# Low limbs of gathered tokens: one one-hot matrix and a copy by ScalarE, in place of a second one-hot matrix and a third product

## The chip, the cores and the metric

The kernel runs on one core of a Trainium2 chip. A core has TensorE (PE: matrix products into PSUM), VectorE (DVE), ScalarE (ACT), GpSimd (POOL) and SyncE (SP), whose queue here issues the transfers (DMA) from main memory. Each engine works through its own list of instructions in order and waits on semaphores for the others. The metric is the time of one execution on the device in microseconds (us); lower is better. Before the change it is 1878.24 us, the median of 3 runs (1877.51 to 1880.09).

## The reference, cut to what matters

A two-layer network on 256 latent tokens of width 1024, with 256 context tokens. The second layer ends in a mixture of eight experts, and the change lies there:

```
logits = (t @ w_router).astype(float32)          # t: 256 tokens x 1024
topv, topi = lax.top_k(logits, 2)
wts = softmax(topv, axis=-1)
combine = sum(wts[..., None] * one_hot(topi, 8), axis=1)
y = zeros_like(t)
for e in range(8):
    y = y + combine[:, e:e + 1] * ((silu(t @ w_g[e]) * (t @ w_u[e])) @ w_d[e])
```

w_g and w_u are 1024 x 3584 for each expert, w_d is 3584 x 1024, all in float32. After it come a gated residual and a final RMSNorm.

## The kernel before, in words

**Limbs.** Products of float32 values are made from two rounded parts: a value is its high limb (what is left of it in the fast product format) plus its low limb (the rest). A product of two tensors is then three products: high with high, low with high, high with low. For weights a load brings 1 MB, a unit, into a buffer `raw`; ScalarE writes the high limbs `eh` (line 1362, `Flow.high`) and VectorE the low limbs `el` = raw - eh (line 1386, `Flow.low`). When a unit's low limbs are made, its buffer is given back (`Flow.release`) and SyncE's queue may issue the next load. `Flow.take(look)` is called by each unit's products: it makes sure of that unit's limbs, and has `look` units more split in advance.

**Tokens of an expert.** The kernel gathers the tokens that go to an expert as the columns of a tile `xh` (with low limbs in `xlo`; for some experts both are halves of one tile `x`), 128 columns wide, with a product by a one-hot matrix `d` (`gather`, line 1443): th (high limbs of all tokens) times `d`, and tl (low limbs) times `d`. When an expert has at most 64 tokens (`FEW`), columns 64 to 127 of `xh` hold the low limbs of the same tokens, so one product with `xh` does the work of two; the two halves of the result are added later (`fold`, and line 1997 for the activations). With more than 64 tokens there is a separate product with `xlo`. For the low limbs in those columns the kernel builds a second one-hot matrix `dl`, with the positions moved by 64 and only for experts with few tokens, and adds the product tl times `dl` to the same result. The later transposed matrix `dT`, with which an expert's output is scattered back to the tokens, is made from `dl` + `d` (line 1479), so that it has the one of each token twice.

The choice between few and many is made while the kernel runs: the counts are loaded into registers of PE, DVE and ACT (`load_count`), and `tc.If(tokens[e] > FEW)` makes a branch on these engines, also on one that has nothing to do inside. In the profile, experts 3, 5 and 6 run the separate product with `xlo`, and the other five don't.

**Order.** Experts run in turn; each has four blocks of its hidden width (1024, 1024, 1024, 512), and a block takes gate units, up units, and the down units of the block before it. Gathers are generators that are advanced a step at a time between units (`bgq["attn"]`, `tick`): expert 1's during expert 0, those of 2 and 3 together during expert 1, of 4 and 5 during expert 3, of 6 and 7 during expert 5. A step makes one chunk's product: four of the eight rows of 128 features for one expert, two for a pair. The first gather is the exception: its steps stand by hand, some ahead of the first unit, some inside it (`mid`, between a unit's high and low products) and behind it.

Of the kernel before, what the change touches and what calls it, by code (L numbers as in the profile page):

```python
# [11 lines left out]
F32 = mybir.dt.float32  # L12
# [3 lines left out]
OP = mybir.AluOpType  # L16
# [59 lines left out]
def hybrid_kernel(ctx, tc, x, c, ctx_in, c_ctx, w_mod, b_mod, norm1_g, norm2_g, w_in, sink, w_fourier,  # L76
# [1347 lines left out]
    w_shift = cmp[:, 0]  # L1424
    d0, dl0 = (rawx.tile([128, 2, 128], F32R, name=nm, bufs=1) for nm in ("d0", "dl0"))
    xl = xT[:, :, 256:512].rearrange("p c (t i) -> p c t i", t=2)
# [7 lines left out]

    def one_hot(d, e, low=False):
        at, on = (posl, sel_few) if low else (pos, sel)
        for t in range(2):
            V.tensor_scalar(d[:, t, :], slot, at[:, t, e:e + 1], on[:, t, e:e + 1],
                            op0=OP.is_equal, op1=OP.mult)
# [3 lines left out]
    def gather(es, base, info):  # L1443


        d, dl, w = d0, dl0, 128 * len(es)
        if es[0] > 1 or base:
            d, dl = (ex.tile([128, 2, 256], F32R, name=nm, tag=tag, bufs=1) for nm, tag in
                     (("d", "ych"), ("dl", "ycl")))
        if es[0] or base:  # L1450
            for i, e in enumerate(es):
                one_hot(d[:, :, i * 128:i * 128 + 128], e)
                if not base:
                    one_hot(dl[:, :, i * 128:i * 128 + 128], e, True)
        yield
# [6 lines left out]
        nk = 512 // w  # L1462
        of = ([(th, d)] + ([] if base else [(tl, dl)]), [(tl, d)])
        for ch in range(0, KC, nk):
            for l in range(2):
                p = psB.tile([128, nk, w], F32, name="pg", tag="t", bufs=2)
                for src, dd in of[l]:
                    for k in range(nk):
                        for t in range(2):
                            P_.matmul(p[:, k, :], src[:, t, (ch + k) * 128:(ch + k + 1) * 128], dd[:, t, :w],  # L1470
                                      start=(src is of[l][0][0] and k + t == 0),
                                      stop=(src is of[l][-1][0] and k + t == nk))
                for i, e in enumerate(es):
                    A.activation(info[e]["x"][l][:, ch:ch + nk, :], p[:, :, i * 128:i * 128 + 128], AF.Copy)  # L1474
                yield
        if base:
            dl = d
        else:
            V.tensor_tensor(dl[:, :, :w], dl[:, :, :w].bitcast(F32), d[:, :, :w].bitcast(F32), op=OP.add)
        if late_weights:  # L1480
# [5 lines left out]
        for i, e in enumerate(es):  # L1486
            di = dl[:, :, i * 128:i * 128 + 128].bitcast(F32)
            p = psB.tile([128, 512], F32, name="pd", tag="t", bufs=2)
            for t in range(2):
                P_.transpose(p[:, t * 128:(t + 1) * 128], di[:, t, :], ident)  # L1490
            for t in range(2):
                P_.matmul(p[:, 256:257], di[:, t, :], comb[:, t, e:e + 1], start=(t == 0), stop=(t == 1))
            dT = ex.tile([128, 256], F32R, name="dT", tag="dT", bufs=3)
            cs = mp.tile([128, 1], F32, name="cs", tag="cs", bufs=3)
            A.activation(dT, p[:, 0:256], AF.Copy)
            A.activation(cs, p[:, 256:257], AF.Copy)
            info[e].update(dT=dT, cs=cs)
            yield

    with ExitStack() as st:  # L1500
# [33 lines left out]
        def row(dst, dg):  # L1534
# [16 lines left out]
        tl = mp.tile([128, 2, D], F32R, name="tl")  # L1551
        sel, comb, rank, sel_few = (mp.tile([128, 2, NE], F32, name=nm) for nm in
                                    ("sel", "comb", "rank", "sel_few"))
        posl = rank
        most = mp.tile([128, 1], I32, name="most")
# [3 lines left out]
        pos = at_of[:, 0:2, :]  # L1559
        few = mp.tile([128, NE], F32, name="few")  # L1560
        gate_cols(1, 2, 0.5, 1)
# [100 lines left out]
        normed(0)  # L1662
        V.tensor_scalar(few, at_of[:, 2, :], FEW + 0.5, None, op0=OP.is_lt)
        V.tensor_scalar(posl, pos, 64.0, None, op0=OP.add)
        V.tensor_tensor(sel_few, sel, few[:, None, :].to_broadcast([128, 2, NE]), op=OP.mult)
        one_hot(dl0, 0, True)
        low_limbs(0)
# [4 lines left out]
        next(g0)  # L1672
        load_count(0)
        next(g0)
        flow.high()
# [11 lines left out]
    with ExitStack() as st:  # L1687
# [121 lines left out]
        def experts(base, flow):  # L1809
# [88 lines left out]
            for j in range(end + 1):  # L1898
                if j < end:
# [3 lines left out]
                    if j == NB and base == 0:  # L1903
                        bgq["attn"].append(rows_of_gates())
                    if b == 1 and e + 1 < NE and base == 0:
                        load_count(e + 1)
                    if j == 2:
# [9 lines left out]
                    for br, ps in enumerate((pg, pu)):  # L1917
                        nu = KC // nk
                        for q in range(nu):
                            unit(e, [(ps[:, h:h + 512], q * nk + k, k * wd + h)  # L1920
                                     for k in range(nk) for h in range(0, wd, 512)],
                                 xh, xlo, q == 0, q == nu - 1, 0 if j == 0 and br == 0 and q == 0 else 2,
                                 br or j == 0 or q < nu - 1,
                                 (lambda: next(g)) if j == 0 and br == 0 and q < 2 and not base else None)
                            if j == 0 and br == 0:
                                if q == 0 or base and q == 1:
                                    next(g)
# [102 lines left out]
```

## Time and profile before

| | |
|---|---|
| median of 3 runs | 1878.24 us |
| profiled execution, its time | 1877.18 us |
| its span (first to last instruction) | 1875.5 us |
| busy: PE, DVE, ACT | 1790.7, 1517.4, 1143.0 us |
| products `dl` with tl | 80 |

The span is 1.7 us shorter than the execution's time. In a timeline row the columns are: start, length, engine, line, operation, out<-in, shapes, count, and in brackets how long the engine was idle before it and what ended that. Rows of one operation that follow each other are merged, and products are pipelined, so their lengths overlap; the distance between two starts is what a group took. PEclk in a row of stretches is the granted TensorE clock: 1.00 is 2.4 GHz and 0.50 is 1.2 GHz. A row of waits gives who waited for whom, the total in us, how often, and the longest.

### The profile page before, as it was taken

To read this page: it belongs to the slowest core of one execution; us is meant where nothing else is said; L and a number is where in the kernel's file an instruction comes from. 1 tells how busy PE (TensorE), PEld (TensorE's weight loads), DVE (VectorE), ACT (ScalarE), POOL (GpSimd) and SP (SyncE) were. 2 spreads that over 40 slices of the span, in tenths; PEclk is the share of its full clock that TensorE was granted. 3 is DMA by queue.
4 is the path that set the end of the run, shared out by engine and by line. 5 is a ranking of instruction groups with operands and counts; after the bars stand their busy time and mean duration, and the time that the engine had idled before them with its cause. 6 is when DMAs were issued, how large, how long until landed. Compare 5 with 4: busy or idle time off the path is not lost. (4 is left out here: it accounts for less than half of the span.)

```text
span 1875.5 us, 27319 instructions
## 1 busy us (share of the span) xinstructions
PE 1790.7 (95%) x9701; PEld 1497.7 (80%) x9701; DVE 1517.4 (81%) x1793; ACT 1143.0 (61%) x1300; POOL 64.3 (3%) x95
## 2 busy tenths in 40 slices
PE   7999999999999999999989999999999999999996
PEld 4788877878888888999878777778887788888874
DVE  6787896577778636787698988999889998888897
ACT  5664623433232224665497877888777887777785
POOL 3200000200000002000000000000000000000000
PEclk9999999999999999999899999999999999999999
DMA  9313462266467422535799999999999999999993
GB/s 295 108 57 102 130 202 95 80 210 199 158 224 249 158 94 85 158 95 209 276 361 339 394 367 361 408 403 408 344 352 405 399 400 327 346 353 375 370 401 123
DMA packets 223312, 488.57 MB, mean 261 GB/s; under 512 B 11426, under 2 KB 107938, under 8 KB 223140
## 3 DMA queue, kind: packets, MB, share of 16 engines
q1 hardware_dynamic: 221860, 482.11, 71.2%
q0 software_dynamic: 1280, 4.20, 0.8%
q8 instruction: 105, 1.72, 0.4%
q14 instruction: 67, 0.55, 0.1%
HBM read 485.22 MB, written 1.05 MB: 259 GB/s over the span
## 5 line engine op out<-in xcount | busy, mean ns | idle before, releaser
L1386 DVE TENSOR_TENSOR el<-raw,eh 128x2048 fp32r<-128x2048 f32 (+2 forms) x332 | 724.0, 2210 | 86.0 <-ACT eh L1362 77.5
L1362 ACT ACTIVATE eh<-raw 128x2048 fp32r<-128x2048 f32 (+2 forms) x332 | 607.8, 1859 | 95.3 <-PE pgt L1843 63.5
L212 PE MATMUL psp<-hh,wh 128*128 128x512 f32 (+1 forms) x704 | 258.9, 368 | 2.6 <-ACT U L965 1.8
L214 PE MATMUL psp<-hh,wl 128*128 128x512 f32 (+1 forms) x704 | 255.1, 362 | 5.4 <-DVE wl L181 5.4
L213 PE MATMUL psp<-hl,wh 128*128 128x512 f32 (+1 forms) x704 | 254.4, 361 | 0.0
L181 DVE TENSOR_TENSOR wl<-raw,wh 128x1024 fp32r<-128x1024 f32 (+1 forms) x152 | 182.4, 1206 | 32.8 <-issue 13.1
L169 ACT ACTIVATE wh<-raw 128x1024 fp32r<-128x1024 f32 (+1 forms) x152 | 156.8, 1039 | 48.8 <-DMA raw<-in_w_down_d 20.4
L214 PEld LDWEIGHTS psp<-hh,wl 128*128 128x128 f32 x704 | 132.9, 189 | 28.3 <-DVE wl L181 8.0
L212 PEld LDWEIGHTS psp<-hh,wh 128*128 128x128 f32 x704 | 133.2, 189 | 25.0 <-issue 2.2
L213 PEld LDWEIGHTS psp<-hl,wh 128*128 128x128 f32 x704 | 133.2, 189 | 19.6 <-issue 0.5
L1843 PE MATMUL py<-el,eah 128*128 128x256 f32 (+1 forms) x712 | 125.9, 315 | 8.6 <-DVE el L1386 7.3
L1843 PEld LDWEIGHTS py<-el,eah 128*128 128x128 f32 x712 | 102.0, 189 | 36.6 <-DVE el L1386 28.3
L1843 PE MATMUL py<-eh,eah 128*128 128x512 f32 x440 | 120.8, 396 | 0.0
L331 DVE SCALAR_TENSOR_TENSOR acc<-rawm,cvec,acc 128x512 f32<-128x512 f32 x140 | 99.8, 746 | 1.3
L1843 PE MATMUL pup<-el,xh 128*128 128x256 f32 (+1 forms) x560 | 93.6, 305 | 4.7 <-DVE el L1386 4.6
L1843 PEld LDWEIGHTS pup<-el,xh 128*128 128x128 f32 x560 | 80.0, 188 | 20.2 <-DVE el L1386 11.5
L1843 PE MATMUL pgt<-el,xh 128*128 128x256 f32 (+1 forms) x480 | 84.5, 314 | 11.2 <-DVE el L1386 10.7
L1843 PE MATMUL pup<-eh,xh 128*128 128x512 f32 x336 | 94.4, 402 | 0.0
L1843 PEld LDWEIGHTS pgt<-el,xh 128*128 128x128 f32 x480 | 69.7, 191 | 27.7 <-DVE el L1386 19.6
L1843 PEld LDWEIGHTS py<-eh,eah 128*128 128x128 f32 x440 | 78.6, 188 | 14.6 <-ACT eh L1362 0.8
L1843 PE MATMUL pgt<-eh,xh 128*128 128x512 f32 x296 | 84.1, 406 | 0.7 <-ACT xh L1474 0.7
L1207 ACT ACTIVATE ah<-af 128x512 fp32r<-128x512 f32 x22 | 13.9, 632 | 95.1 <-DVE af L1206 95.1
(382 smaller groups left out, 3242.6 us busy)
## 6 DMA issues: line engine op xcount, KB each, us to landing
raw<-in_w_gate_e SPq DMA_DIRECT2D x111, 1024.0 KB, 8.1
raw<-in_w_down_e SPq DMA_DIRECT2D x110, 1024.0 KB, 8.3
raw<-in_w_up_e SPq DMA_DIRECT2D x109, 1024.0 KB, 8.8
rawm<-in_w_mod SPq DMA_DIRECT2D x112, 256.0 KB, 4.9
raw<-in_w_in SPq DMA_DIRECT2D x26, 1024.0 KB, 5.5
raw<-in_w_gate_d SPq DMA_DIRECT2D x11, 1024.0 KB, 5.4
raw<-in_w_up_d SPq DMA_DIRECT2D x11, 1024.0 KB, 5.4
mraw<-in_w_mod SPq DMA_DIRECT2D x16, 512.0 KB, 8.5
```

Source lines behind the costliest of these rows:

```text
L169: A.activation(h[:, :n, :], src, AF.Copy)
L181: self.eng.tensor_tensor(lo[:, :n, :], src, h[:, :n, :].bitcast(F32), op=OP.subtract)
L212: P_.matmul(ps, wh[:, k, :], ah, start=(start and i == 0), stop=False)
L213: P_.matmul(ps, wh[:, k, :], al, start=False, stop=False)
L214: P_.matmul(ps, wl[:, k, :], ah, start=False, stop=(stop and i == n - 1))
L331: V.scalar_tensor_tensor(acc[v], r, s, acc[v], op0=OP.mult, op1=OP.add)
L1207: A.activation(ah[:, i, :], t, AF.Copy)
L1362: A.activation(self.like(self.hi[i][:, sl], x), x, AF.Copy)
L1386: V.tensor_tensor(self.like(self.lo[i][:, sl], x), x, self.like(self.hi[i][:, sl], x).bitcast(F32), op=OP.subtract)
L1843: P_.matmul(ps[:, a:b], x[:, k, :], w[:, c + a:c + b], start=(start and ps_id[i] not in seen), stop=(stop and ps_id[i] not in ps_id[i + 1: ...
```

## The change

`dl`, `few`, `sel_few` and the moved positions are gone, with their one-hot steps and the sum of `dl` and `d`. A gather's chunk is now two products, th with `d` and tl with `d`. For the second, ScalarE branches: with many tokens it copies to `xlo` as before; with few it copies the first 64 columns into columns 64 to 127 of `xh`. `dT` and `cs` are written in two halves of 64 rows; with few tokens the second half is a second copy of the first. The counts of experts e+1 and e+2 are now read together in every odd expert, since a pair's gather asks for both. In the first gather, both products of chunk 0 stand ahead of the first unit and those of chunk 1 inside units 0 and 1; the first unit now looks two units ahead, as all others do.

```
-    d0, dl0 = (rawx.tile([128, 2, 128], F32R, name=nm, bufs=1) for nm in ("d0", "dl0"))
+    d0 = rawx.tile([128, 2, 128], F32R, name="d0", bufs=1)
...
                 one_hot(d[:, :, i * 128:i * 128 + 128], e)
-                if not base:
-                    one_hot(dl[:, :, i * 128:i * 128 + 128], e, True)
...
-        of = ([(th, d)] + ([] if base else [(tl, dl)]), [(tl, d)])
...
+            for l, src in enumerate((th, tl)):
...
+                for k in range(nk):
+                    for t in range(2):
+                        P_.matmul(p[:, k, :], src[:, t, (ch + k) * 128:(ch + k + 1) * 128], d[:, t, :w],
+                                  start=(k + t == 0), stop=(k + t == nk))
                 for i, e in enumerate(es):
-                    A.activation(info[e]["x"][l][:, ch:ch + nk, :], p[:, :, i * 128:i * 128 + 128], AF.Copy)
+                    pe, (hi, lo) = p[:, :, i * 128:i * 128 + 128], info[e]["x"]
+                    if l == 0 or base:
+                        A.activation((hi, lo)[l][:, cs_, :], pe, AF.Copy)
+                        continue
+                    with tc.If(tokens[e] > FEW) as many:
+                        A.activation(lo[:, cs_, :], pe, AF.Copy)
+                    with many.Else():
+                        A.activation(hi[:, cs_, 64:128], pe[:, :, 0:64], AF.Copy)
                 yield
-        if base:
-            dl = d
-        else:
-            V.tensor_tensor(dl[:, :, :w], dl[:, :, :w].bitcast(F32), d[:, :, :w].bitcast(F32), op=OP.add)
...
-            di = dl[:, :, i * 128:i * 128 + 128].bitcast(F32)
+            di = d[:, :, i * 128:i * 128 + 128].bitcast(F32)
...
-            A.activation(dT, p[:, 0:256], AF.Copy)
-            A.activation(cs, p[:, 256:257], AF.Copy)
+            def rows(to, src):
+                A.activation(dT[to], p[src, 0:256], AF.Copy)
+                A.activation(cs[to], p[src, 256:257], AF.Copy)
...
+                with tc.If(tokens[e] > FEW) as many:
+                    rows(first, first)
+                    rows(second, second)
+                with many.Else():
+                    rows(first, first)
+                    rows(second, first)
...
         next(g0)
         load_count(0)
+        next(g0)
         next(g0)
...
-                    if b == 1 and e + 1 < NE and base == 0:
-                        load_count(e + 1)
+                    if b == 1 and base == 0:
+                        for e1 in ((1,) if e == 0 else (e + 1, e + 2) if e % 2 and e + 2 < NE else ()):
+                            load_count(e1)
...
-                                 xh, xlo, q == 0, q == nu - 1, 0 if j == 0 and br == 0 and q == 0 else 2,
+                                 xh, xlo, q == 0, q == nu - 1, 2,
...
-                                if q == 0 or base and q == 1:
+                                if base and q < 2:
                                     next(g)
```

What ScalarE has in a row at the first gather and the first units, before (`xh` and `xlo` are copies of the gather's chunks, `th` the high limbs of the second half of the features, the first `eh` is half of unit 1, the last row units 2 and 3 and so on; the branch is a unit's):

```order
L1474 ACTIVATE xh<-pg 128x512
L1362 ACTIVATE eh<-raw 128x1024
L1651 ACTIVATE th<-xa 128x512 x2
L1474 ACTIVATE xlo<-pg 128x512
L1868 COMPARE_AND_BRANCH
L1868 UNCONDITIONAL_BRANCH x2
L1474 ACTIVATE xh<-pg 128x512
L1362 ACTIVATE eh<-raw 128x2048 x2
L1474 ACTIVATE xlo<-pg 128x512
```

The same place on ScalarE, now:

```order
L1470 ACTIVATE xh<-pg 128x512
L1472 COMPARE_AND_BRANCH
L1473 ACTIVATE xlo<-pg 128x512
L1472 UNCONDITIONAL_BRANCH
L1475 ACTIVATE xh<-pg 128x4x64
L1472 UNCONDITIONAL_BRANCH
L1362 ACTIVATE eh<-raw 128x1024
L1657 ACTIVATE th<-xa 128x512 x2
L1362 ACTIVATE eh<-raw 128x2048
L1470 ACTIVATE xh<-pg 128x512
```

The second copy of chunk 0 has come ahead of unit 1's half, and unit 2's `eh` ahead of the copy of chunk 1.

TensorE at the same place, before (`pg` is the gather's result, `pgt` the gate's):

```order
L1470 MATMUL pg<-d_6322,th 128x128 x8
L1470 MATMUL pg<-dl_6323,tl 128x128 x8
L1843 MATMUL pgt<-eh,xh 128x512 x4
L1470 MATMUL pg<-d_6322,tl 128x128 x8
L1868 COMPARE_AND_BRANCH
L1843 MATMUL pgt<-eh,xlo 128x512 x4
L1843 MATMUL pgt<-el,xh 128x512 x4
L1868 UNCONDITIONAL_BRANCH
L1843 MATMUL pgt<-el,xh 128x256 x8
L1868 UNCONDITIONAL_BRANCH
L1470 MATMUL pg<-d_6322,th 128x128 x8
L1470 MATMUL pg<-dl_6323,tl 128x128 x8
```

And now:

```order
L1465 MATMUL pg<-d_6322,th 128x128 x8
L1465 MATMUL pg<-d_6322,tl 128x128 x8
L1472 COMPARE_AND_BRANCH
L1472 UNCONDITIONAL_BRANCH x2
L1846 MATMUL pgt<-eh,xh 128x512 x4
L1465 MATMUL pg<-d_6322,th 128x128 x8
L1871 COMPARE_AND_BRANCH
L1846 MATMUL pgt<-eh,xlo 128x512 x4
L1846 MATMUL pgt<-el,xh 128x512 x4
L1871 UNCONDITIONAL_BRANCH
L1846 MATMUL pgt<-el,xh 128x256 x8
L1871 UNCONDITIONAL_BRANCH
```

Two groups of eight products stand ahead of the first unit as before, but the second is now `d,tl`; inside unit 0 the first of chunk 1 stands in the place of the last of chunk 0; and a branch with no work in it has come onto TensorE.

VectorE at the gather of experts 2 and 3, before:

```order
L1438 TENSOR_SCALAR d<-cols,at_of,sel 128x128 x2
L1438 TENSOR_SCALAR dl<-cols,rank,sel_few 128x128 x2
L1438 TENSOR_SCALAR d<-cols,at_of,sel 128x128 x2
L1438 TENSOR_SCALAR dl<-cols,rank,sel_few 128x128 x2
L1385 COMPARE_AND_BRANCH
L1386 TENSOR_TENSOR el<-raw,eh 128x2048
L1385 UNCONDITIONAL_BRANCH x2
```

And now:

```order
L1437 TENSOR_SCALAR d<-cols,at_of,sel 128x128 x4
L1385 COMPARE_AND_BRANCH
L1386 TENSOR_TENSOR el<-raw,eh 128x2048
L1385 UNCONDITIONAL_BRANCH x2
L1871 COMPARE_AND_BRANCH
```

The four steps of `dl` are gone from the front of the next `el`.

## Rows read from the trace of the kernel before

**Rows 1.** Stretches: busy us and count of PE, PEld, DVE, ACT, POOL; clock; DMA share, GB/s

```profile
944.00:990.00 46.00, 40.80 (x240) 32.58 (x239) 44.33 (x36) 43.02 (x36) 0.00 (x0) 1.00 1.00 377
1262.00:1390.00 128.00, 128.00 (x612) 105.58 (x611) 112.46 (x72) 98.39 (x83) 0.00 (x0) 1.00 0.98 367
1490.00:1750.00 260.00, 260.00 (x1209) 212.32 (x1208) 227.15 (x136) 197.62 (x151) 0.00 (x0) 1.00 0.96 361
```

**Rows 2.** Waits, 900 us and 925 us to the end: the queue's, VectorE's for weights

```profile
SPq L1236 <- DVE el L1386: 682.7, 265, 12.9
...
DVE el L1386 <- DMA raw<-in_w_gate_e: 1.8, 2, 1.4
```

**Rows 3.** Timeline of TensorE at the first gather and units 0 to 3

```profile
929.34 2.07 PE L1843 MATMUL pgt<-eh,xh 128*128 128x512 f32 x4 [0.75 <-ACT xh L1474]
931.21 1.80 PE L1470 MATMUL pg<-d,tl 128*128 128x128 f32 x8
932.81 2.00 PE L1843 MATMUL pgt<-el,xh 128*128 128x256 f32 x8
934.62 1.03 PE L1470 MATMUL pg<-d,th 128*128 128x128 f32 x8
935.49 1.06 PE L1470 MATMUL pg<-dl,tl 128*128 128x128 f32 x8
...
941.36 1.21 PE L1843 MATMUL pgt<-el,xh 128*128 128x256 f32 x8 [1.10 <-DVE el L1386]
942.40 1.10 PE L1843 MATMUL pgt<-eh,xh 128*128 128x512 f32 x4
```

**Rows 4.** Timeline of ScalarE and of VectorE at the same place

```profile
930.13 1.14 ACT L1651 ACTIVATE th<-xa 128x512 fp32r<-128x512 f32 x2
...
937.07 3.71 ACT L1362 ACTIVATE eh<-raw 128x2048 fp32r<-128x2048 f32 x2
...
939.01 6.70 DVE L1386 TENSOR_TENSOR el<-raw,eh 128x2048 fp32r<-128x2048 f32 x3 [5.99 <-ACT eh L1362]
```

**Rows 5.** Stretches at the start and after the second gather

```profile
926.00:934.00 8.00, 7.25 (x31) 6.68 (x31) 5.73 (x10) 3.18 (x5) 0.00 (x0) 0.50 0.17 38
...
940.00:944.00 4.00, 2.84 (x17) 2.06 (x16) 4.00 (x3) 4.00 (x4) 0.00 (x0) 1.00 0.62 199
1010.00:1018.00 8.00, 7.44 (x44) 6.29 (x45) 6.48 (x6) 8.00 (x8) 0.00 (x0) 1.00 0.55 186
```

**Rows 6.** Timeline of TensorE and ScalarE at the gather of expert 1

```profile
991.42 1.06 PE L1470 MATMUL pg<-dl,tl 128*128 128x128 f32 x8
992.31 3.70 PE L1843 MATMUL pgt<-raw,xh 128*128 128x172 f32 x24
...
992.51 0.60 ACT L1474 ACTIVATE xh<-pg 128x512 fp32r<-128x512 f32 x1 [2.48 <-PE pg L1470]
```

**Rows 7.** Timeline of three engines where the gather of 2 and 3 ends

```profile
1133.32 0.68 DVE L1479 TENSOR_TENSOR dl<-dl,d 128x512 fp32r<-128x512 f32 x1
...
1134.15 0.41 PE L1490 MATMUL pd<-ident,dl 128*128 128x128 f32 x2 [2.96 <-DVE dl L1479]
...
1134.94 0.39 ACT L1495 ACTIVATE dT<-pd 128x256 fp32r<-128x256 f32 x1 [2.65 <-PE pd L1492]
...
1138.55 0.38 ACT L1495 ACTIVATE dT<-pd 128x256 fp32r<-128x256 f32 x1 [1.36 <-PE pd L1492]
```

**Rows 8.** Timeline of TensorE in expert 3

```profile
1343.80 0.64 PE L1470 MATMUL pg<-dl,tl 128*128 128x256 f32 x4
1344.27 1.08 PE L1843 MATMUL pup<-eh,xh 128*128 128x512 f32 x4
1345.19 1.09 PE L1843 MATMUL pup<-eh,xlo 128*128 128x512 f32 x4
1346.13 1.10 PE L1843 MATMUL pup<-el,xh 128*128 128x512 f32 x4
```

**Rows 9.** Line 1868, a unit's branch: operation, count, duration ns min/median/max, starts

```profile
L1868 PEldq COMPARE_BRANCH  x430: 65/202/438, 929.4 to 1854.5; - x144
```

More of the change, by code (lines that the diff above doesn't have):

```diff
@@ L1433, in hybrid_kernel, with one_hot @@
                     compare_op=OP.is_equal, fill=0.0)
-    def one_hot(d, e, low=False):
-        at, on = (posl, sel_few) if low else (pos, sel)
+    def one_hot(d, e):
         for t in range(2):
-            V.tensor_scalar(d[:, t, :], slot, at[:, t, e:e + 1], on[:, t, e:e + 1],
+            V.tensor_scalar(d[:, t, :], slot, pos[:, t, e:e + 1], sel[:, t, e:e + 1],
                             op0=OP.is_equal, op1=OP.mult)
@@ L1443, in gather @@
     def gather(es, base, info):
-        d, dl, w = d0, dl0, 128 * len(es)
+        d, w = d0, 128 * len(es)
         if es[0] > 1 or base:
-            d, dl = (ex.tile([128, 2, 256], F32R, name=nm, tag=tag, bufs=1) for nm, tag in
-                     (("d", "ych"), ("dl", "ycl")))
+            d = ex.tile([128, 2, 256], F32R, name="d", tag="ych", bufs=1)
         if es[0] or base:
@@ L1462, in gather @@
         nk = 512 // w
-        of = ([(th, d)] + ([] if base else [(tl, dl)]), [(tl, d)])
         for ch in range(0, KC, nk):
-            for l in range(2):
+            cs_ = slice(ch, ch + nk)
+            for l, src in enumerate((th, tl)):
                 p = psB.tile([128, nk, w], F32, name="pg", tag="t", bufs=2)
[L1467 to L1472, printed above, removed]
-                for i, e in enumerate(es):
-                    A.activation(info[e]["x"][l][:, ch:ch + nk, :], p[:, :, i * 128:i * 128 + 128], AF.Copy)
+                for k in range(nk):
+                    for t in range(2):
+                        P_.matmul(p[:, k, :], src[:, t, (ch + k) * 128:(ch + k + 1) * 128], d[:, t, :w],
+                                  start=(k + t == 0), stop=(k + t == nk))
+                for i, e in enumerate(es):
+                    pe, (hi, lo) = p[:, :, i * 128:i * 128 + 128], info[e]["x"]
[6 more added lines that the diff above has]
+                        A.activation(hi[:, cs_, 64:128], pe[:, :, 0:64], AF.Copy)
                 yield
-        if base:
-            dl = d
-        else:
-            V.tensor_tensor(dl[:, :, :w], dl[:, :, :w].bitcast(F32), d[:, :, :w].bitcast(F32), op=OP.add)
         if late_weights:
@@ L1494, in gather @@
             cs = mp.tile([128, 1], F32, name="cs", tag="cs", bufs=3)
-            A.activation(dT, p[:, 0:256], AF.Copy)
-            A.activation(cs, p[:, 256:257], AF.Copy)
+            def rows(to, src):
+                A.activation(dT[to], p[src, 0:256], AF.Copy)
+                A.activation(cs[to], p[src, 256:257], AF.Copy)
+            first, second = slice(0, 64), slice(64, 128)
+            if base:
+                rows(slice(0, 128), slice(0, 128))
+            else:
+                with tc.If(tokens[e] > FEW) as many:
[4 more added lines that the diff above has]
+                    rows(second, first)
             info[e].update(dT=dT, cs=cs)
@@ L1551, in hybrid_kernel @@
         tl = mp.tile([128, 2, D], F32R, name="tl")
-        sel, comb, rank, sel_few = (mp.tile([128, 2, NE], F32, name=nm) for nm in
-                                    ("sel", "comb", "rank", "sel_few"))
-        posl = rank
+        sel, comb, rank = (mp.tile([128, 2, NE], F32, name=nm) for nm in ("sel", "comb", "rank"))
         most = mp.tile([128, 1], I32, name="most")
@@ L1559, in hybrid_kernel @@
         pos = at_of[:, 0:2, :]
-        few = mp.tile([128, NE], F32, name="few")
         gate_cols(1, 2, 0.5, 1)
@@ L1662, in hybrid_kernel @@
         normed(0)
[L1663 to L1666, printed above, removed]
         low_limbs(0)
```

## Prediction

> **What bounds the kernel now.** I read the stages first. The busy time by stretch [rows 1] shows three regimes in the experts' part (from 924 us to the end). In 944 to 990 us, where expert 0 runs on at most 64 tokens, VectorE is busy 44.33 of 46.00 us and ScalarE 43.02; TensorE has gaps. In 1262 to 1390 and 1490 to 1750, where experts 3, 5 and 6 run on more than 64 tokens, TensorE is busy without any gap, 128.00 of 128.00 and 260.00 of 260.00. The transfers are near their limit in all of them (share 0.96 to 1.00), so the next question is who waits for whom. The waits answer it [rows 2]: the queue that issues the weights waited 682.7 us for VectorE's low limbs to free a buffer, and the largest wait of a computing engine for weights is 1.8 us in all. So the engines set the pace and the transfers follow; what is saved on the leading engine of a stretch moves the end, as long as the transfers can follow.
>
> **The start of expert 0** is the first place. TensorE's timeline [rows 3] shows the first gather between the units: eight products of 128 columns each for the high limbs (`d,th`), for the low limbs behind them (`dl,tl`) and for the low limbs alone (`d,tl`). In front of unit 2's low product TensorE stands 1.10 us until `el` comes at 941.36; VectorE had itself been idle 5.99 us, waiting for ScalarE's `eh`, which stood behind the copy of `xh` and came at 937.07 [rows 4].
>
> Now by parts, from 929.34, where unit 0 starts. Before it, `d,tl` takes the place that `dl,tl` had, so the start of unit 0 stays (its copy is smaller; the new wait for the second copy, which writes columns 64 to 127 of `xh`, lies where the wait of 0.75 us for the first was). After it, the 1.60 us of `d,tl` (931.21 to 932.81) are taken by chunk 1's `d,th`, at the same granted clock of 0.50 (1.2 GHz) that this stretch has [rows 5]. The old `d,th` at 934.62 and the `dl,tl` at 935.49 are gone: 935.49 - 934.62 = 0.87 each, 1.74 together. The wait of 1.10 goes because unit 2's `eh` now stands ahead of chunk 1's copy: ScalarE is free of `th` at 931.3 (930.13 + 1.14 [rows 4]), so `eh` is done near 933.2 and `el` 2.3 us later, some 3 us before TensorE asks for it. What could be late next is chunk 1's second copy, behind which unit 2 and all that follows on TensorE would queue; unit 1's `el` product, 1.04 us like unit 2's (941.36 to 942.40), lies between and covers its 0.4 us. Unit 3 moves from 942.40 to 942.40 - 1.74 - 1.10 = 939.6: **2.8 us**. The ends: 0 if the copies come late in turn, 5.9 if VectorE's 5.99 us of idling were all won. I take the TensorE sum, since each row of it is there. ScalarE and VectorE run nearly full behind it [rows 1], so the shift is handed on. The transfers can follow in part: their share is 0.62 in 940 to 944, 1.5 us idle, because the next issue waits for unit 2's `el` [rows 5].
>
> **The copies of `dT`.** Four instead of two per expert, the second pair 64 rows each. A `dT` takes 0.39 us [rows 7], whatever its rows, and its `cs` lies in its tail, so 0.4 more. For expert 0 ScalarE is full: -0.4. For the others it lies in waits or beside a full TensorE.
>
> **Gather of expert 1**, 990 to 1010. ScalarE waits 2.48 us for the gather's products [rows 6], and the `eh` behind that copy wait with it. Two chunks each lose `dl,tl`: 992.31 - 991.42 = 0.89, so **1.8 us**. The transfers idle (1 - 0.55) x 8 = 3.6 us right after it [rows 5], so they have room for it. Ends: 0 if ScalarE's two new branches and copies eat it; 2.5 if VectorE's sum of `dl`, of the size of the 0.68 in rows 7, counts on top.
>
> **Gather of experts 2 and 3**, 1102 to 1146. Here the sum of `dl` and `d` stood on VectorE at 1133.32, behind a low limb and a product; TensorE waited 2.96 us for it, and ScalarE's `dT` 2.65 us and 1.36 us [rows 7]. In the changed kernel `d` is transposed, which is there from the gather's start. What is late next is ScalarE itself: two more pairs (0.8), eight branches of copies and two of `dT` (0.4 at 0.04 each), and the products that it still has to wait for (a few tenths). 2.65 + 1.36 - 0.8 - 0.4 - 0.5 = 2.3; of the gather's own matmuls (four times about 0.47 us) and the one-hots I count 0.3, because ScalarE copies without a pause there. **2.6 us**; ends 0 and 4.9 (the wait of 2.96 and 1.9 of matmuls).
>
> **Gathers in experts 3 and 5**, where TensorE is full. A chunk's `dl,tl` takes 1344.27 - 1343.80 = 0.47 us; four chunks, 1.9 us in each [rows 8]. Ten `If`s are added in each, and every one is passed by TensorE too, though it copies nothing. What one costs there: 1344.27 to 1345.19 holds four products and an `If`, 0.92; 1345.19 to 1346.13 holds four without, 0.94. So nothing that can be seen; I charge 0.04 each, 0.4. **1.5 us** twice. Ends: 0 and 1.9 each.
>
> The two token counts read together in experts 1, 3 and 5 instead of one in each expert are as many loads as before: nothing.
>
> Sum: 2.8 - 0.4 + 1.8 + 2.6 + 1.5 + 1.5 = 9.8 us. The profiled execution took 1877.18, 1.06 below the median of 1878.24; 1877.18 - 9.8 = 1867.4, and at the median's level **1868.4 us**.
>
> **A page that speaks against it.** The branch rows: the pair at L1868 was passed 430 times, TensorE's compare taking 202 ns in the median and 438 at most, ahead of its work [rows 9]. The Trainium skill, Runtime: NRT & Kernel Launch, section Instruction fetch mechanics, says that a taken branch whose target is not among the pages held has to wait for a fetch before it goes on. By that rule the `If`s would cost far more than 0.04; rows 8 do not bear it out for bodies this short, and the second rival below is what it would do here. The skill's Advanced Engine Details and Errata, Control Flow Timing, gives about 108 ns for a compare and 51 for a plain branch; as an estimate by that page, twenty of these on a full TensorE would be 3.2 us in place of 0.8 and the time some 1870.8, where rows 8 show no such step.
>
> **Rivals.**
> 1. The transfers cap the early part. For it: their share is 1.00 in 944 to 990, so the 6.8 us gained before expert 3 must come out of transfer idling (1.5 + 3.6 us [rows 5]) or out of the lead that loaded buffers have. Against it: the waits for weights are next to nothing now [rows 2]. If only 3 of these 6.8 us are kept, the sum is 6.0: 1872.2. Chance 0.20.
> 2. The `If`s decide: slower. There are 36 (three each for experts 0 and 1, ten for each of three pairs), all on TensorE, ScalarE and VectorE in order. Without what I charged (0.4 twice and 0.4) the gain is 11.0, so it turns at 11.0 / 36 = 0.31 us each. At the longest recorded compare, 0.438 on TensorE [rows 9], 36 are 15.8 us: 4.8 slower, 1883.0. For it: the bodies hold work now and end in a jump. Against it: rows 8. Chance 0.05.
> 3. TensorE's clock comes back later. It was at 0.50 from 926 to 934 [rows 5], after a pause, and rose while TensorE worked nearly without gaps. With less work between the units, new pauses could keep it down some 6 us longer; at half speed that costs 3: 1871.4. Chance 0.10.
> 4. More than forecast: VectorE's idling at the start and the stall at 1131 are both won whole, 5.9 + 4.9 in place of 2.8 + 2.6: 1863.0. Chance 0.10.
>
> The forecast keeps 0.55, with its own range of 1865 to 1871.5. The range of 1862.5 to 1874.5 takes in rivals 1, 3 and 4 and leaves out the slower case. A change of under 0.2% (3.8 us, 1874.5) can't be told from none in a measurement of this kernel. Faster than that: nearly all of the forecast, rivals 3 and 4 and four fifths of rival 1, less a share for what I have not seen, 0.84; within it 0.11; slower 0.05.
>
> **What would show it.** Right: no `dl` in the profile, 80 products fewer; unit 3 of expert 0 near 939.6 and no wait for `el` at unit 2; the transfers' share near 1 in 940 to 944; no stall at the transposes of experts 2 and 3; the full stretches of experts 3 and 5 each 1.5 us shorter. Wrong: ScalarE or VectorE waiting for weights before expert 3 (rival 1); steps of some tenths of a microsecond at the new branches (rival 2); a granted clock of 0.50 past 934 (rival 3).

## The result and the profile after

The changed kernel took 1868.13 us, the median of 4 runs (1865.29 to 1868.37), beside 1879.16 for the kernel before: ratio 0.9942, interval 0.993 to 0.9954. Timed again beside the experiments it took 1864.62 (5 runs) against 1878.57, ratio 0.9928, interval 0.9915 to 0.9941. By the medians of the two sets the change is worth 11 and 14 us. The profiled execution took 1868.02 with a span of 1866.2; there is no `dl` in it, and TensorE runs 9621 instructions, 80 fewer.

Before the stages can be compared, one thing has to be taken out. TensorE's first product of the first gather started at 924.46 in the profile before; after, its row in TensorE's timeline is

```profile
928.31 0.48 PE L1465 MATMUL pg<-d,th 128*128 128x128 f32 x1 [2.31 <-DVE xa L1655]
```

That is 3.85 us later, though the same instructions stand ahead of it. It is the execution, not the change: over thirteen profiles (all kernels below) this start lies anywhere from 923.47 to 929.97. So all that follows is counted from this product.

**The start of expert 0** answers to [rows 3 to 5]. TensorE's timeline after:

```profile
932.96 2.07 PE L1846 MATMUL pgt<-eh,xh 128*128 128x512 f32 x4 [0.53 <-ACT xh L1475]
934.83 1.87 PE L1465 MATMUL pg<-d,th 128*128 128x128 f32 x8
936.50 2.02 PE L1846 MATMUL pgt<-el,xh 128*128 128x256 f32 x8
938.31 1.91 PE L1846 MATMUL pgt<-eh,xh 128*128 128x512 f32 x4
940.02 1.70 PE L1465 MATMUL pg<-d,tl 128*128 128x128 f32 x8
941.56 1.15 PE L1846 MATMUL pgt<-el,xh 128*128 128x256 f32 x8
942.55 1.09 PE L1846 MATMUL pgt<-eh,xh 128*128 128x512 f32 x4
943.48 1.11 PE L1846 MATMUL pgt<-el,xh 128*128 128x256 f32 x8
944.43 1.10 PE L1846 MATMUL pgt<-eh,xh 128*128 128x512 f32 x4
```

No row waits for `el` any more. Unit 3 starts at 944.43, which is 940.58 on the clock of before. But unit 0 and the high products of unit 1 (938.31 to 940.02) run at half speed, where before had full speed from the end of unit 0 (934.62) on. The stretches show it (busy us and count of PE, PEld, DVE, ACT, POOL, then clock, DMA share, GB/s):

```profile
928.00:941.00 13.00, 11.97 (x46) 10.71 (x46) 10.54 (x14) 8.16 (x10) 0.00 (x0) 0.50 0.51 180
941.00:944.00 3.00, 3.00 (x21) 2.82 (x21) 0.93 (x1) 2.11 (x2) 0.00 (x0) 0.92 1.03 400
```

**The gathers.** Expert 1's [rows 6] and the end of that of experts 2 and 3 [rows 7], ScalarE's and TensorE's rows after:

```profile
993.48 0.60 ACT L1470 ACTIVATE xh<-pg 128x512 fp32r<-128x512 f32 x1 [1.60 <-PE pg L1465]
...
1010.51 0.37 ACT L1493 ACTIVATE dT<-pd 64x256 fp32r<-64x256 f32 x1
1010.77 0.16 ACT L1494 ACTIVATE cs<-pd 64x1 f32<-64x1 f32 x1
1010.94 0.38 ACT L1493 ACTIVATE dT<-pd 64x256 fp32r<-64x256 f32 x1
1011.22 0.15 ACT L1494 ACTIVATE cs<-pd 64x1 f32<-64x1 f32 x1
1011.39 3.71 ACT L1362 ACTIVATE eh<-raw 128x2048 fp32r<-128x2048 f32 x2
...
1129.58 0.38 PE L1487 MATMUL pd<-ident,d 128*128 128x128 f32 x2
...
1130.89 0.40 ACT L1493 ACTIVATE dT<-pd 64x256 fp32r<-64x256 f32 x1
```

The wait of 2.48 is 1.60; the doubled copies of expert 1's `dT` stand between limbs and take 1011.39 - 1010.51 = 0.88 us with no pause; and the stall of 2.96 at the transposes is gone, with ScalarE's 2.65 behind it.

**The full stretches** [rows 1, 8] and the weights [rows 2]. TensorE's products and the waits of VectorE after:

```profile
1340.56 0.72 PE L1465 MATMUL pg<-d,tl 128*128 128x256 f32 x4
1341.12 1.09 PE L1846 MATMUL pup<-eh,xh 128*128 128x512 f32 x4
1342.05 1.09 PE L1846 MATMUL pup<-eh,xlo 128*128 128x512 f32 x4
```

```profile
DVE el L1386 <- DMA raw<-in_w_down_e: 2.7, 2, 1.4
```

The unit behind a chunk steps by 0.93 as before, and VectorE's wait for weights, 2.7 us in all and the only one of this kind, is as small as before, where 1.8 was the largest. That the transfers would cap the early part did not happen.

### The profile page after: what moved, and what is told of

It is laid out like the page before. It is cut to its first block, busy times and chain, and to the rows that moved or that the text cites. A ratio compares the mean times of both kernels' runs of the same rounds, so it can differ in the third digit from the quotient of the medians.

```text
span 1866.2 us, 27317 instructions
## 1 busy us (share of the span) xinstructions
PE 1783.0 (96%) x9621; PEld 1492.2 (80%) x9621; DVE 1509.7 (81%) x1769; ACT 1145.2 (61%) x1316; POOL 63.6 (3%) x95
## 5 line engine op out<-in xcount | busy, mean ns | idle before, releaser
L1846 PE MATMUL pgt<-el,xh 128*128 128x256 f32 (+1 forms) x480 | 84.5, 314 | 10.9 <-DVE el L1386 10.5
```

The source lines that it names most:

```text
L1846: P_.matmul(ps[:, a:b], x[:, k, :], w[:, c + a:c + b], start=(start and ps_id[i] not in seen), stop=(stop and ps_id[i] not in ps_id[i + 1: ...
```

## The experiments

To follow a gain through the kernel I take, in each profile, the first product of the first gather (`pg<-d,th`) and the starts of the activations `sg<-pgt`, one in each of the 32 blocks, and subtract. In before:

```profile
952.50 1.03 ACT L1935 ACTIVATE sg<-pgt 128x1024 f32<-128x1024 f32 x1
```

lies 952.50 - 924.46 = 28.04 us behind the product, and after,

```profile
953.78 1.03 ACT L1939 ACTIVATE sg<-pgt 128x1024 f32<-128x1024 f32 x1
```

953.78 - 928.31 = 25.47: 2.56 us gained with the unrounded starts. The table has these differences against the profile of before (us, negative is sooner; "3.1" is expert 3's second block; the last row is the end of the span):

| at | before again | after | after again | look0 | dT from d | keep sum | ifs split | twice d | before warm | warm | warm look0 | warm twice |
|---|---|---|---|---|---|---|---|---|---|---|---|---|
| 0.0 | +0.10 | -2.56 | -3.38 | -2.53 | +1.59 | -2.70 | -2.23 | -3.80 | -4.08 | -7.51 | -6.34 | -7.51 |
| 0.1 | +0.10 | -2.56 | -3.38 | -2.52 | +1.58 | -2.68 | -2.23 | -3.80 | -4.08 | -7.51 | -6.34 | -7.51 |
| 0.2 | +0.13 | -4.06 | -4.90 | -4.03 | +2.14 | -4.73 | -2.87 | -5.33 | -4.08 | -9.04 | -7.87 | -9.02 |
| 0.3 | +0.14 | -3.50 | -4.33 | -3.48 | +2.69 | -4.73 | -2.32 | -5.32 | -4.10 | -8.49 | -7.33 | -9.02 |
| 1.2 | +0.11 | -4.84 | -5.69 | -4.82 | +2.67 | -5.79 | -3.21 | -6.71 | -4.11 | -9.82 | -8.65 | -10.41 |
| 1.3 | -1.43 | -8.73 | -9.57 | -8.72 | -1.11 | -5.80 | -7.01 | -10.60 | -4.07 | -13.70 | -12.55 | -14.29 |
| 3.1 | -1.41 | -8.68 | -9.53 | -8.67 | -1.04 | -5.81 | -6.96 | -10.56 | -4.07 | -13.65 | -12.48 | -14.21 |
| 3.3 | -1.40 | -10.94 | -11.78 | -10.94 | -1.06 | -7.21 | -8.89 | -12.84 | -4.05 | -15.92 | -14.76 | -16.49 |
| 4.3 | -1.39 | -10.60 | -11.47 | -10.65 | -1.04 | -7.20 | -8.84 | -12.84 | -4.02 | -15.63 | -14.44 | -16.48 |
| 5.3 | -1.40 | -12.81 | -13.64 | -12.83 | -0.93 | -8.62 | -10.74 | -15.00 | -4.01 | -17.80 | -16.61 | -18.65 |
| 7.3 | -1.41 | -12.83 | -13.64 | -12.83 | -0.94 | -8.62 | -10.74 | -15.00 | -4.03 | -17.77 | -16.54 | -18.62 |
| end | -2.04 | -13.10 | -13.47 | -12.58 | -1.51 | -8.85 | -11.27 | -15.43 | -4.12 | -18.15 | -16.74 | -17.95 |

Two executions of one kernel agree from block to block within some 0.1 us. They differ at the start of expert 0, in how the product's own start lies, at the gather of 2 and 3 for the kernel before (row 1.3), and by up to 0.7 us at the very end. In the four kernels with ten extra products ahead of the gather (the last columns) those products can hold up the product that the table counts from; see before warm.

**After again** and **before again** (no edit).

> The changed kernel once more, beside the other versions. Between the two profiles the first product of the first gather starts 3.85 us later after the change (924.46 before, 928.31 after), although no instruction ahead of it differs; from there to the end of the span it is 951.0 us before and 937.9 after, 13.1 shorter, of which 9.3 are left at the end. Theory: those 3.85 us belong to the one execution and not to the change; the stretch from that product to the end is 937.9 again within 1 us, and the start of that product lies somewhere in 924 to 929. Rival: the changed kernel is later there every time, and the start is again within 0.5 us of 928.3.

> The kernel before once more, with a profile of its own. The version that only takes dT from d has the same instructions up to the end of the first gather and still left the start of expert 0 1.59 us later than the profile of before did. Theory: how long the first gather and the first units take varies by some 2 us between executions, with the moment at which TensorE's clock comes back after the pause (10 to 17 us behind the first product in the profiles so far); behind that the stretches agree within 0.1 us. So: from the first product to the end 950 to 954, the difference arising before the first activation of expert 0. Rival: the kernel before holds 951.0 within 0.3 us, and the 1.59 us are something that the edit does.

After again started the first gather at 924.12, not at 928.3, and took 937.53 us from there to the end where the first profile has 937.90. So the 3.85 us belong to the execution; the rival falls. Before again has a start of 28.14 us, 0.10 from before, so the kernel before did not vary there as I expected; that of "dT from d" (+1.59), with the same instructions, did. The start goes with the moment at which TensorE's clock comes back to 1.00, read from stretches of one us: 10.2 us behind the product in before, 10.4 in before again and 17.1 in dT from d; 10.5 in twice d (-3.80), 11.4 in after again (-3.38) and 13.2 in after (-2.56), which have the same instructions at the start. The stretch of the return in after again, and then in twice d, whose product starts at 924.96:

```profile
932.00:936.00 4.00, 4.00 (x18) 3.67 (x18) 3.28 (x6) 3.02 (x3) 0.00 (x0) 0.55 0.94 324
```

```profile
932.00:936.00 4.00, 4.00 (x19) 3.81 (x19) 3.57 (x6) 3.60 (x3) 0.00 (x0) 0.57 0.78 241
```

So at a like moment of return (before and twice d) the change is worth 3.8 us at the start, and the 2.56 of the first profile are what a later return left of it.

What I had not expected is that before again is 1.5 us shorter at another place, the gather of 2 and 3. The stall is the same:

```profile
1137.82 0.41 PE L1490 MATMUL pd<-ident,dl 128*128 128x128 f32 x2 [2.97 <-DVE dl L1479]
```

but the clock behind it is not. The eight us behind the stall in before, and then in before again:

```profile
1134.46:1138.46 4.00, 4.00 (x24) 3.82 (x23) 2.98 (x2) 2.25 (x3) 0.00 (x0) 0.70 0.85 274
1138.46:1142.46 4.00, 4.00 (x24) 3.53 (x23) 2.68 (x2) 3.91 (x4) 0.00 (x0) 0.87 0.96 333
```

```profile
1138.01:1142.01 4.00, 4.00 (x29) 3.66 (x28) 2.99 (x2) 3.12 (x6) 0.00 (x0) 1.00 0.80 278
1142.01:1146.01 4.00, 4.00 (x31) 3.77 (x30) 3.75 (x3) 3.76 (x4) 0.00 (x0) 1.00 0.95 320
```

The same pause costs 1.5 us more where TensorE's clock falls behind it (mean 0.79) than where it stays at 1.00.

**dT from d** (before, with one part of the change):

```
-            V.tensor_tensor(dl[:, :, :w], dl[:, :, :w].bitcast(F32), d[:, :, :w].bitcast(F32), op=OP.add)
...
-            di = dl[:, :, i * 128:i * 128 + 128].bitcast(F32)
+            di = d[:, :, i * 128:i * 128 + 128].bitcast(F32)
```

and the two halves of `dT` and `cs` with their branch, and the reading of the counts, as in the change.

> The kernel before, in which only the scatter matrices dT are made from d (two halves of 64 rows, with the branch), and the sum of dl and d is gone; the second one-hot matrix and the third product stay. Theory: nearly all of the 5.2 us that the gather of experts 2 and 3 gained comes from the stall at the transposes (2.96 us) and from the clock that no longer sags behind it (0.79 in eight us, about 1.7): that gather gains some 4.5, the doubled copies of dT cost some 0.6 in expert 0, the rest stays; from the first product of the gather to the end some 947 us where before has 951.0, ratio 0.998. Rival, the forecast's own account: ScalarE is what is late next there, the stall is worth 2.3: some 949. Rival: the fewer products were what counted, the gather gains nothing: 951.5.

1875.42 against 1878.57, ratio 0.9987 (0.9978 to 0.9996). From 0.3 to 1.3 it goes from +2.69 to -1.11: 3.80 us at the gather of 2 and 3, where I expected 4.5 and the forecast's account was 2.3. Against before again, which has no sag (-1.43 - 0.14 = -1.57 there), 2.23 are left: the forecast's figure. No row waits at the transposes:

```profile
1132.70 0.38 PE L1486 MATMUL pd<-ident,d 128*128 128x128 f32 x2
```

and the clock of the stretch behind it is 1.00:

```profile
1133.47:1137.47 4.00, 3.68 (x23) 2.97 (x23) 4.00 (x4) 3.93 (x11) 0.00 (x0) 1.00 0.98 357
```

My total of 947 was missed (949.49), since its start was 1.59 us late and the copies of `dT` cost 0.56 us in expert 0 and again 0.55 in expert 1 (rows 0.2 and 0.3), where I had counted one.

**Keep sum** (the changed kernel, with that part undone: `dl`'s one-hots, the sum and whole copies of `dT` are back; the third product stays out).

> The changed kernel, in which dT is again made from the sum of dl and d: the second one-hot matrix is built and the sum made on VectorE, and dT copied whole; the third product stays out. It is the counterpart of the version that only takes dT from d. Theory: it loses about 4.5 us at the gather of experts 2 and 3, where the transposes wait for the sum again, and wins some 0.6 back in expert 0: from the first product of the first gather to the end some 942 us where the changed kernel has 937.9; experts 3 and 5 keep their 2.2 us each. Rival (the fewer products gave the 5.2 us): 937.5 to 938.5.

1869.99, ratio 0.9954 (0.9941 to 0.9966), against the changed kernel's 0.9928; 942.15 us from the product to the end, as the theory said. The gather of 2 and 3 gains only 1.07 (-4.73 to -5.80), all of it ahead of the stall, which is back with its sagging clock:

```profile
1133.78 0.56 PE L1495 MATMUL pd<-ident,dl 128*128 128x128 f32 x2 [3.31 <-DVE dl L1484]
```

```profile
1131.97:1135.97 4.00, 2.19 (x9) 1.99 (x10) 3.87 (x3) 0.94 (x3) 0.00 (x0) 0.76 1.01 382
1135.97:1139.97 4.00, 4.00 (x25) 3.64 (x24) 2.29 (x1) 2.52 (x4) 0.00 (x0) 0.82 0.84 287
```

A miss: experts 3 and 5 keep 1.40 and 1.42 of their 2.26 and 2.21. TensorE's first chunk in expert 3 stretches over the extra one-hots on VectorE, as in before, whose row is the first here, and a low limb comes late:

```profile
1325.35 0.88 PE L1470 MATMUL pg<-d,th 128*128 128x256 f32 x4
...
1325.05 0.87 PE L1469 MATMUL pg<-d,th 128*128 128x256 f32 x4
1328.02 1.19 PE L1849 MATMUL pgt<-el,xh 128*128 128x512 f32 x4 [0.22 <-DVE el L1386]
```

Where the one-hots are gone that chunk takes 0.63. So 0.24 + 0.22 of the 0.86 are seen; the rest was not followed.

**Look0** (the first unit has no unit split ahead):

```
-                                 xh, xlo, q == 0, q == nu - 1, 2,
+                                 xh, xlo, q == 0, q == nu - 1, 0 if j == 0 and br == 0 and q == 0 else 2,
```

> The changed kernel, in which the first unit again has no unit split ahead (the order of ScalarE's high limbs at the start as before; the products and copies of the gather stay as changed). Theory: the wait for the low limb at unit 2 or 3 comes back, and the 2.6 us that the start of expert 0 gained fall to 1 to 1.6: from the first product to the end some 939.2 us where the changed kernel has 937.9. Rival: the start is set by TensorE at half clock (to about 941.5 us) and by the matmuls alone, the order of ScalarE makes no difference: 937.9.

1864.53, ratio 0.9924, no different from the changed kernel; the first block at -2.53 beside -2.56. The two can be compared, since the clock came back at the same moment (13.3 us behind the product, 13.2 in after). The rival holds: with the clock at 0.50 that long the order of ScalarE's limbs makes no difference, and no row of units 0 to 3 waits for `el` with the old order either.

**Ifs split** (twice as many branches):

```
+                    for a, b in ((ch + z, ch + z + 1) for z in range(nk)):
...
+                            A.activation(lo[:, a:b, :], pk, AF.Copy)
```

> The changed kernel, in which each copy of the gathered low limbs is cut into one of each row of features, each with its own branch: 36 branches more than the 36 there are (6 each for experts 0 and 1, 8 for each pair), and as many small copies on ScalarE. Theory (the forecast, as the runs so far leave it): a branch costs a full TensorE nothing that can be seen; the gathers in experts 3 and 5, 8 branches more in each, lose 0 to 0.3 us each. Where ScalarE is full its smaller copies cost about 0.4 us a chunk: expert 0 0.8, expert 1 0.8, the gather of 2 and 3 1 to 1.6. Rival (branches decide): 0.31 us each or more, 2.5 us in each of experts 3 and 5, 7.4 and more in all.

1868.86, ratio 0.9949 (0.9935 to 0.9962). Experts 3 and 5 lose 0.33 and 0.31 against the changed kernel, not 2.5 each; the gather of expert 1 loses 0.86, as expected, and that of 2 and 3 0.5, half of what I expected. By the two ratios the kernel is some 4 us slower than the changed one; were all of it the branches', the 36 would cost 0.11 us each, a third of what the rival needed. And on a full TensorE the branches themselves show no step. The chunks in expert 3 with split copies, and in the changed kernel:

```profile
1331.38 0.62 PE L1465 MATMUL pg<-d,tl 128*128 128x256 f32 x4
1338.30 0.64 PE L1465 MATMUL pg<-d,th 128*128 128x256 f32 x4
1341.71 0.72 PE L1465 MATMUL pg<-d,tl 128*128 128x256 f32 x4
1345.06 0.63 PE L1465 MATMUL pg<-d,th 128*128 128x256 f32 x4
```

```profile
1330.22 0.62 PE L1465 MATMUL pg<-d,tl 128*128 128x256 f32 x4
1337.14 0.64 PE L1465 MATMUL pg<-d,th 128*128 128x256 f32 x4
...
1343.91 0.63 PE L1465 MATMUL pg<-d,th 128*128 128x256 f32 x4
```

The distances are 6.92, 3.41 and 3.35 with twice the branches, and 6.92, 3.42 (1340.56 above) and 3.35. The 0.3 us in expert 3 lies at one place, the second chunk (3.58 in place of 3.26), and not at every branch; why it lies there was not followed.

**Warm** (the changed kernel with work for TensorE in the pause; its result isn't read):

```
+        warm = psB.tile([128, 512], F32, name="warm", tag="t", bufs=2)
+        for _ in range(10):
+            P_.matmul(warm[:, 0:128], ident, ident, start=True, stop=True)
         g0 = gather([0], 0, info0)
```

> The changed kernel with ten products of the identity by itself, whose result nobody reads, in the pause of TensorE ahead of the first gather (926.0 to 928.3 in the profile after). Theory: TensorE's granted clock then stays at 1.00 where it is at 0.50 for 11 to 13 us from the first product; TensorE sets the pace there (ScalarE waits 1.90, 1.11 and 2.21 us for its products), so the first activation of expert 0 comes 2 to 4 us sooner: 934 to 936 from the first product to the end where the changed kernel has 937.9 and 937.5. Rival: at full clock ScalarE and VectorE set the pace, under 0.7 us is won. Rival, slower: the products run on past th and hold the first gather up, 0.5 us lost. If the clock falls in spite of them, nothing is learnt on the first two.

1859.81 us, ratio 0.9906 (0.9891 to 0.9921), and 932.85 us from the product to the end. The clock held, and the first activation comes 7.51 us sooner than before, 4.1 to 5.0 sooner than in the two profiles of the changed kernel, more than I expected:

```profile
924.00:932.00 8.00, 6.97 (x48) 5.86 (x48) 7.57 (x12) 6.56 (x9) 0.00 (x0) 1.00 0.32 86
```

**Before warm** and **warm look0** (the same ten products in the kernel before, and in the changed kernel with look0's order).

> The kernel before with the same ten products of the identity in TensorE's pause ahead of the first gather. With the clock at 1.00 on both sides the start of expert 0 can be compared without the luck of its return. Theory: at full clock ScalarE and VectorE set the pace of the first units; the four products taken from the path are worth only half of the 2.8 us of the forecast, but the wait at unit 2 for its low limb is longer, since TensorE comes there sooner: from the first product to the first activation of expert 0 (28.04 us before, 20.5 in the changed kernel with these products) some 23 to 24, so that the change is worth 2.5 to 3.5 us there. The time is some 4 us below before. Rival: the change's gain at the start is only that of products at half clock: 21 to 21.5. Rival: the clock falls in spite of the products, since the kernel before has a longer wait at unit 2.

> The changed kernel with the ten products, in which the first unit has no unit split ahead. Without the ten products this order made no difference at the start (first activation 2.53 us sooner than before, the changed kernel 2.56 and 3.38), with TensorE at half clock. Theory: at full clock the order of ScalarE's high limbs counts, because VectorE and ScalarE then set the pace: the first activation of expert 0 comes 0.5 to 2 us later than in warm (7.51 sooner than before). Rival: the order makes no difference at either clock: within 0.2 us of warm.

The table has -4.08 for the kernel before at the start, but its time falls by 2.2 only (1875.82, ratio 0.999, 0.9981 to 0.9999), not by the 4 I expected. Two things show in its rows. The clock fell in spite of the products, from about 924.8 to 928.2, as the second rival had it:

```profile
923.14:927.14 4.00, 3.63 (x23) 3.57 (x23) 3.60 (x13) 1.60 (x3) 0.00 (x0) 0.71 1.05 377
927.14:931.14 4.00, 3.25 (x21) 3.02 (x21) 3.14 (x5) 1.41 (x2) 0.00 (x0) 0.87 0.06 19
```

And its ten products run on to the very product that the table counts from. In before that product comes 1.46 us behind VectorE's `xa` (924.46 - 923.00), in before warm 2.86 us. The first row is before's, the others are before warm's:

```profile
923.00 1.40 DVE L1649 SCALAR_TENSOR_TENSOR xa<-xa,rstd,both 128x512 f32<-128x512 f32 x2
...
923.80 3.69 PE L1673 MATMUL warm<-ident 128*128 128x128 f32 x20 [0.37 <-DVE at_of L1659]
924.28 1.41 DVE L1649 SCALAR_TENSOR_TENSOR xa<-xa,rstd,both 128x512 f32<-128x512 f32 x2
927.14 1.60 PE L1470 MATMUL pg<-d,th 128*128 128x128 f32 x8
```

So I count from `xa` too, which no product of TensorE here holds up: the first activation comes 2.69 us sooner than before in before warm and 7.18 in warm (where the product comes 1.79 behind an `xa` at 922.51). With the ten products on both sides the change is then worth 3.43 us by the product and 4.49 by `xa`; since before warm's clock is at 1.00 only from 928.2 on, this is a range and not a measurement at one clock.

ScalarE's order can be read more plainly, as warm and warm look0 both have the clock at 1.00 from the product on (warm look0: 1861.05 us, ratio 0.9917, 0.9903 to 0.993): 7.51 - 6.34 = 1.17 us. So the order counts at full clock and not in after and look0, where the clock is at 0.50 for 13 us. That VectorE and ScalarE set the pace at full clock, and TensorE at half clock, fits this; it is my reading of it. The wait that the forecast spoke of is there in before warm:

```profile
939.95 1.21 PE L1846 MATMUL pgt<-el,xh 128*128 128x256 f32 x8 [1.08 <-DVE el L1386]
```

**Twice d** and **warm twice** (VectorE makes the one-hot of each token twice, where the count is few; `dT` is copied whole for all but expert 0):

```
+                    with tc.If(tokens[e] > FEW) as many:
+                        one_hot(d[:, :, i * 128:i * 128 + 128], e)
+                    with many.Else():
+                        one_hot(d[:, :, i * 128:i * 128 + 128], e, twice)
```

> The changed kernel, in which for expert 1 and the pairs VectorE branches at the one-hot matrix: with few tokens it compares the positions with 0..63 twice over, so that d itself has the one of each token twice; ScalarE's second copy then overwrites columns 64 to 127 as before, and dT and cs are copied whole, with no branch and no second pair (expert 0 keeps them). Theory: the second pair of copies and its branch costs ScalarE 0.55 us wherever it is full, in expert 1 as in expert 0, so expert 1 gains 0.55 us, the gather of 2 and 3 up to 0.6, and nothing is lost on VectorE, whose one-hots are as many: 936.8 to 937.4 from the first product to the end, beside 937.9 and 937.5. Rival: the branches ahead of the one-hots hold VectorE up in experts 1 to 3 by what ScalarE wins: no difference.

> The changed kernel with both: the ten products in the pause ahead of the first gather, and for expert 1 and the pairs the one-hot matrix with each token twice. The two edits lie at different places (start of expert 0; end of the gather of expert 1 and scatter of expert 4), and the gains should add: 4 to 5 us and 0.9 us. Theory: from the first product to the end some 932 us (warm alone 932.9), from the first activation of expert 0 on 11.1 to 11.2 us shorter than before, 0.99 of before's time. Rival: what the start gains the transfers take back where the one-hots no longer leave ScalarE a pause: no better than warm alone.

Twice d took 1863.76, ratio 0.993 (0.9916 to 0.9943), in its time no different from the changed kernel. In the profile the 0.56 us of expert 1 are not lost (-5.33 to -5.32 from 0.2 to 0.3), since ScalarE has one pair of copies there, 0.32 us to the next limb:

```profile
1005.89 0.38 ACT L1501 ACTIVATE dT<-pd 128x256 fp32r<-128x256 f32 x1
1006.15 0.18 ACT L1502 ACTIVATE cs<-pd 128x1 f32<-128x1 f32 x1
1006.21 3.73 ACT L1362 ACTIVATE eh<-raw 128x2048 fp32r<-128x2048 f32 x2
```

The gather of 2 and 3 gains nothing more (5.28 us beside 5.23). That its 935.57 us from the product on lie below the expected 936.8 comes from its start (-3.80), where the clock came back as early as in before. With both edits the gains add up to the end of expert 7 (-18.62 beside warm's -17.77), but the time, 1861.06 and ratio 0.9909 (0.9896 to 0.9923), can't be told from warm's. Warm, warm look0 and warm twice are the fastest kernels of the study and can't be told apart by their times, and the second edit is not shown to help.

## Why the prediction was right, and where its steps were not

The time of 1868.4 us came out (1868.13), in part by luck: the sum of 9.8 us was some 3 too small. From the first product on the profile is 13.1 us shorter, but it began its experts 3.85 us later than before's did, and the second set of runs (1864.62) lies 14 below before. By its steps:

- **Start of expert 0, 2.8:** 2.56 and 3.38 in the two profiles, 3.80 in twice d's, where the clock came back as in before. Unit 3 came at 940.58 for the forecast's 939.6, 1.8 us gained; in twice d 3.06. So the size was near, and nearer in the first profile than it would have been at a like clock. Half of the reason was right: unit 2's wait for `el` goes, but not by the order of ScalarE's limbs, as the forecast had it, since at the clock that the start really had it goes without that order too (look0). Rival 3's sign was there (0.50 to 941) beside the forecast's gain. That the change causes the later return is not shown: dT from d, which has the old work between the units, had the latest one of all.
- **Copies of dT, -0.4:** 0.56 in expert 0, and the same again in expert 1. The step "for the others it lies in waits" failed for expert 1: its copies stand in the middle of ScalarE's limbs.
- **Gather of expert 1, 1.8:** 1.50 net of expert 0's `dT`, 2.06 without; keep sum, which has no second pair, shows 2.05.
- **Gather of 2 and 3, 2.6:** the term that was mis-sized. It gained 5.23 against before (-3.50 to -8.73) and 3.66 against before again (less 1.57). From block 1.2 to 1.3, where the stall lies, it is 3.89 and 2.35 (less 1.54): so the stall itself, with ScalarE's new copies taken off, was worth the 2.3 that I gave it. Two other things were missed: the clock's sag behind the stall, 1.5 us that were in the profile I read from, though not in the rows that I showed, and are not in every execution; and the gather's own products and one-hots, taken as 0.3 because ScalarE copies there without a pause, which were worth 1.34 (-3.50 to -4.84), 1.06 of it by the products (keep sum).
- **Experts 3 and 5, 1.5 each:** 2.26 and 2.21. The 0.4 charged for branches in each was not seen, and the wait of the first chunk for VectorE's one-hots, which the rows shown did not hold, went too (0.88 to 0.63). The Trainium skill, Advanced Engine Details and Errata, Control Flow Timing, gives 108 ns for a compare and 51 for a branch; as an estimate by that page ten would cost a full TensorE 1.6 us, and the distances above disagree.
- **Not in the sum:** 0.34 us lost in expert 4 (-10.94 to -10.60). Look0, warm and warm look0 lose it too; twice d, warm twice, keep sum, dT from d and ifs split don't. In after it lies where one high limb of ScalarE, at 1432.84, waits 0.27 us for a down product; before has no wait there. I have no cause for it.

Rival 1 (transfers) and rival 2 (branches) did not occur; rival 4 came near in its size (13.1 for 15.2, and the second set's 1864.62 for its 1863.0), though by other terms than it named.

## What to carry to other kernels

Compare two profiles from a common mark ahead of the change, not from zero, and take a second profile of each side where a stage's clock is below 1.00. A stall's price holds the clock that sags behind it, and that part is there only in some executions; what is taken away ahead of a stall counts beside it. And a pause in front of a stage that TensorE leads can be worth filling: on top of the change, ten products that nobody reads were worth some 4 us, the one-hot matrix made twice nothing that its time shows. In the kernel before the same ten products gained 2.2 us only, since there the clock fell in spite of them and they held the gather up.

## What the runs showed of the hardware

TensorE's clock behind one and the same pause of 2.96 or 2.97 us fell in before (0.70 and 0.87 in the next eight us) and stayed at 1.00 in before again; in before warm, with the same pause, it fell too (0.70 in 1134 to 1138).

At the start of the experts the clock had fallen to 0.50 by 1 us behind the first product in all nine profiles without the ten products. It came back between 932 and 936 in after again, where the gather began at 924.12, and only behind 941 in after, where it began at 928.31, with the same instructions. In dT from d it was still at 0.50 in 932 to 940, where TensorE was busy for all of the 8.00 us. The Trainium skill, TensorE: Matmul & The Clock Gate, Part 1, says that the point of return differs from run to run; the traces agree, and here it differs by more than the half microsecond that the section names: from 10.5 to 13.3 us behind the product with the start of the change, from 10.2 to 17.1 with the old one.

What the half clock costs at this place is some 4 us of this kernel's time, as much as the largest part of the change: from `xa` to the first activation warm takes 3.8 and 4.6 us less than the two profiles of the changed kernel. Ten products of 128 columns, some 2.5 us, kept the clock at 1.00 in all three kernels that have them on top of the change, and not in before warm.
